# Moving the SBUF pools of a one-core gMLP + SSD block so that the operand tiles begin at multiples of 512 bytes

## The chip, the cores and the metric

The kernel is written for one Trainium2 chip and runs on one of its cores. The core has a matrix engine (TensorE, PE in the profile; its weight loads are listed as PEld), three engines for elementwise work (VectorE = DVE, ScalarE = ACT, GpSimd = POOL) and a queue engine (SyncE = SP) that issues most of the loads; ScalarE issues most of the stores. The metric is the device time of one execution in microseconds. The kernel before takes 1429.13 us, the median of three runs (1428.83 to 1432.63).

## What is computed

One layer over a sequence of 1024 tokens with 1024 features, in float32. The sequence is normalised and modulated, multiplied by a wide input matrix, and its column blocks feed two branches: a gated spatial mixer (y_a) and a chunked state-space scan (SSD, y_b). Both are projected, gated, added, projected once more and normalised.

```
h = rms_norm(x, norm_w) * (1 + scale) + shift        # shift, scale, gate from silu(c) @ ada_w + ada_b
gm_u, gm_v, gm_z, ssm_z, xbc, dt_raw, g_a, g_b = split(h @ w_in)      # 11296 columns
y_a = spatial_gating(gelu(gm_u), gelu(gm_v), ...) * silu(gm_z)
xs, bm, cm = split(silu(causal_depthwise_conv(xbc)))
dt = softplus(dt_raw + dt_bias);  a = -exp(a_log)
y_b = rms_norm((ssd_scan(xs, dt, a, bm, cm) + xs * d_skip) * silu(ssm_z))
merged = sigmoid(g_a) * (y_a @ w_proj_a) + sigmoid(g_b) * (y_b @ w_proj_b)
out = rms_norm(x + gate * (merged @ w_out), final_norm_w)
```

The vectors dt_bias, a_log and d_skip, 32 numbers each (one for each SSD head), are the ones whose tiles the change moves.

## The kernel before

**Products.** The large products are made from two-part operands: a float32 value is split into a rounded high part (type fp32r, which the matrix engine takes in one pass) and a low part, and three products of parts are added (high by high, high by low, low by high). A matmul multiplies a stationary operand of 128x128 (512 bytes on each partition), loaded into the array ahead of it, by a moving operand of 128x512 (2048 bytes on each partition). In the trace the names on the right of the arrow give both, as in xz<-t3h,p7z2h: t3h moves, p7z2h stands still.

**Stages**, in order of time on the core:

1. 0 to 75 us, the first stage. `first_products` (lines 351 to 361) multiplies the first 288 columns while h is made. Its tiles live in the pool p0. The queue's order there is written out: at the second step (n == 1), after the loads of the next modulation block and weights, lines 449 to 451 load dtb, abc and dsk, each a broadcast of 32 numbers to 128 partitions. dsk is read once, in `small_parameters` (line 431), to make dskt.
2. 75 to 930 us, the rest of the input matrix in pairs of column blocks. `product` (line 573) issues 12 matmuls with one of the operands of h (b11, t1, t2, b22, t3, b21, t4; pool hp) moving and one of the weight blocks (pool wp) standing. A pair has seven products. Small tasks are put between products by `later` and `run_tasks`: a task given a delay of n runs n products on. One chain of such tasks, `dt_part1` to `dt_part3`, starts after 216 products: it loads dt_raw back from memory (dtt, line 648), adds dtb (line 663) and, some products later, exponentiates abc (line 690) and multiplies by it (line 692).
3. 930 to 1168 us, the SSD scan, with the projection of y_a (`proj_a`, tile pma) drawn in between in small portions. The order of all engines is written out here (the flag `hand`).
4. 1168 to 1345 us, the projection of y_b: `multiply` (line 1525), 56 units of 12 matmuls. The moving parts (named ..bh and ..bl) are in hp; the stationary blocks (named ..a) come from `big`, which takes 4096-byte places in the pools p2r and p2q.
5. 1345 to 1431 us, the output product (`out_product`, tile po). Its moving operand (woh, wol) is in hp. Its stationary parts come from `m_slot`: fifteen of the 32 lie in five tiles of tag sl (pools p2r and p2q; they appear as mmh and mml), seventeen in single places of hp (mh and ml).

**Pools.** SBUF is laid out as two stacks. The left one grows upward: const, then hp (56 tiles of 2048 bytes), then p0, whose place is taken by wp and wsp (16 and 8 tiles of 2048 bytes) once the first stage is over. The right one grows downward from the top: w4 (six tiles of 4096 bytes), then gm and gx; gx gives way to the pool pre, and later w4, gm and pre give way to p2r, p2x and p2q, which reach down over the places of wsp and wp. A tile that takes a place must wait until those who used the place before are done (`reuse_waits`). The operations that aren't pinned to program order are put in order by the framework's scheduler.

**Where tiles begin.** In the program before, ident, the first tile of const, begins 128 bytes past a multiple of 512. Const holds six tiles of 512 bytes (ident, ones, tri, par, par2, cwt), four of 1024 (dthq, dde, nacs, cd) and small ones: nhalf 32, dtb 128, abc 128, dskt 64, dsk 128, sc 32, ssq 256. That is 7936 bytes, and 128 + 7936 is 384 past a multiple of 512. So hp, and after it wp and wsp, whose tiles all have 2048 bytes, begin 384 past a multiple of 512. The top of the right stack is at 480 past a multiple of 512, and so are all its tiles of 4096, 2048 and 1024 bytes.

Of the kernel before, what the change touches and what calls it, by code (L numbers as in the profile page):

```python
# [8 lines left out]
F32 = mybir.dt.float32  # L9
# [7 lines left out]
P = 128  # L17
# [6 lines left out]
NH = 32  # L24
# [11 lines left out]
def hybrid_kernel(  # L36
# [47 lines left out]
    def cst(shape, name, dt=F32):  # L84
        return const.tile(shape, dt, name=name, tag=name)
# [9 lines left out]
    def f32(t):  # L95
        return t.bitcast(F32)

    def load(dst, src):
        pin(nc.sync.dma_start(dst, src))
# [23 lines left out]
    par = cst([P, P], "par")  # L123
    par2 = cst([P, P], "par2")
    cwt = cst([P, P], "cwt")
    dtb = cst([P, NH], "dtb")
    abc = cst([P, NH], "abc")
    dskt = cst([P, 16], "dskt")
    dsk = cst([P, NH], "dsk")
    sc = cst([P, KT], "sc")  # L130
    dthq = cst([P, NCH * NH], "dthq")
    dde = cst([P, NCH * NH], "dde")
# [30 lines left out]
    def last_split(nm):  # L163
# [2 lines left out]
        pin(A.copy(hi, t))  # L166
        pin(V.tensor_sub(lo, t, f32(hi)))

    w4pool = tc.tile_pool(name="w4pool", bufs=1, side="right", reuse_waits="tile")
    w4p = w4pool.__enter__()  # L170
    w4 = [w4p, 6]

    def wide(name, dt=F32):
        return w4[0].tile([P, S], dt, name=name, tag="w4", bufs=w4[1])


    with tc.tile_pool(name="p0", bufs=1, reuse_waits="tile") as p0:
# [8 lines left out]
        def aw_tile(n):  # L186
            return p0.tile([P, KT, 2, P], F32, name=f"aw{n}", tag="aw", bufs=2)

        hf2 = {}

        def hf_tile(k, h):
# [18 lines left out]
        def load_aw(n):  # L210
            k = KS[n]
            if n:
                aw[n] = aw_tile(n)
            for j in range(2):
                load(aw[n][:, :, j, :],
                     ada_w[:, j * D + k * P : j * D + (k + 1) * P].rearrange("(k p) c -> p k c", p=P))

        def load_w0(n):
            k = KS[n]
            raw = p0.tile([P, W0], F32, name=f"w0r{n}", tag="w0r", bufs=2)  # L220
            wd = p0.tile([P, 2 * NH], F32R, name=f"w0d{n}", tag="w0d", bufs=2)
            hi, lo = (p0.tile([P, 256], F32R, name=f"w0{v}{n}", tag=f"w0{v}", bufs=2) for v in "hl")
            load(raw, w_in[k * P : (k + 1) * P, COL_DT : COL_DT + W0])
            wk[n] = (raw, wd, hi, lo)

        def split_w0(n):
            raw, wd, hi, lo = wk[n]
            pin(A.copy(hi, raw[:, NH:W0]))
            pin(A.copy(wd[:, 0:NH], raw[:, 0:NH]))
            pin(V.tensor_sub(lo, raw[:, NH:W0], f32(hi)))  # L230
            pin(V.tensor_sub(wd[:, NH:], raw[:, 0:NH], f32(wd[:, 0:NH])))
# [119 lines left out]
        def first_products(n):  # L351
            raw, wd, wh, wl = wk[n]
            for h in halves(n):
                hh, hl = hhs[n, h]
                for m, (lw, r) in enumerate(((wh, hh), (wl, hh), (wh, hl))):
                    for i in (1, 2):
                        mm(accs[i][h], lw[:, i * P - P : i * P], r, n + m == 0, n == KT - 1 and m == 2)
                        yield
                for nd, r in ((2 * NH, hh), (NH, hl))[:: 1 if n == 0 else -1]:
                    mm(accs[0][h][0:nd, :], wd[:, 0:nd], r, n == 0 and r is hh, n == KT - 1 and r is hh)  # L360
                    yield
# [46 lines left out]
        def prepare(n):  # L408

            if n == 1:  # L410
                return {
                    8: lambda: (warm(6), transposes(0, 1), rows_of_h(0, 1), matvec(1), warm(5)),
                    11: lambda: (transposes(1, 1), modulation(1), rows_of_h(1, 1)),
                    16: lambda: (transposes(1, 0), rows_of_h(1, 0)),
                }
            a, b = halves(n)
            return {
                2: lambda: (matvec(n), transposes(n, a)),
                6: lambda: (modulation(n), rows_of_h(n, a)),
                14: lambda: (transposes(n, b), rows_of_h(n, b)),  # L420
            }

        def small_parameters():
            pp = ax("pp1")
            for i in range(2):
                tp(pp[:, i * P : (i + 1) * P], pkb[:, i], ident)
            for i in range(2):
                pin(V.tensor_copy((par2, cwt)[i], pp[:, i * P : (i + 1) * P]))
            for hh in range(2):
                part = slice(hh * HD, (hh + 1) * HD)  # L430
                pin(V.tensor_copy(dskt[part, :], dsk.rearrange("p (i h) -> p i h", h=2)[part, :, hh]))
# [10 lines left out]
        for n in range(KT):  # L442
            todo = prepare(n + 1) if n + 1 < KT else {}
            for at, _ in enumerate(first_products(n), 1):
                if at == 1 and n + 2 < KT:
                    load_aw(n + 2)
                    load_w0(n + 2)
                if at == 1 and n == 1:
                    load(dtb, dt_bias.to_broadcast([P, NH]))
                    load(abc, a_log.to_broadcast([P, NH]))  # L450
                    load(dsk, d_skip.to_broadcast([P, NH]))
                if at in todo:
                    todo[at]()
                for f, kk in sums.get((n, at), ()):
                    f(kk)
                if at == 2 and 0 < n < KT - 1:
                    split_w0(n + 1)
                if n == 4 and at == 8:
                    small_parameters()
# [7 lines left out]
    gm = gmpool.__enter__()  # L467
# [23 lines left out]
    def later(delay, f, *a):  # L491
        tasks.append((slot[0] + delay, f, a))
# [143 lines left out]


    bsb = gm.tile([P, D], F32, name="bsb", tag="bsb")
    first_c1 = {"v0": gx.tile([P, S], F32, name="c1v0", tag="wst")}
    wst = None  # L640
    bst = gx.tile([P, NCH, NG, 6], F32, name="bst", tag="bst")
# [3 lines left out]
    def dt_part1():  # L645

        dtt = wide("dtt2")[0 : 2 * NH, :]
        load(dtt, dt_d)
        V.tensor_add(fold[0], ident[:, 0:NH], ident[:, NH : 2 * NH])
        sm1 = wide("sm1").rearrange("p (a n) -> p a n", a=4)  # L650
        sm2 = wide("sm2").rearrange("p (a n) -> p a n", a=4)
        later(2, dt_part1a, dtt, sm1, sm2)
# [522 lines left out]
    def stats():  # L1175
        v_stats()
        mix_load(0)

    later(216, dt_part1)
    later(9, mix_weights)  # L1180
    for i in range(4):
# [586 lines left out]
```

## Time and profile before

| | us |
|---|---|
| median of three runs | 1429.13 |
| the profiled execution, whole | 1432.24 |
| its span, first to last instruction | 1430.5 |
| PE busy within the span | 1400.6 (98%), 7087 matmul records |
| DVE busy | 1027.8 (72%) |
| ACT busy | 782.0 (55%) |
| POOL busy | 204.9 (14%) |

The span is what the trace shows; the profiled execution's own time is 1.7 us longer than it, and 3.1 us longer than the median of the runs. In the trace a matmul's duration runs from its start to a modelled end, and successive matmuls overlap, so a duration is not a pace. The pace is read from starts: a row of the timeline gives the start of a group, its length and how many instructions it merges, and from the start of one group to the start of a later one, divided by the number of matmuls between, is the time that one takes. A granted clock (PEclk) of 1.00 means that the matrix engine was not throttled in that stretch.

### The profile page before, as it was taken

The numbers are of one execution on the slowest core, as the hardware profiler recorded it, in microseconds if no ns is written. First come the engines' busy times: TensorE is split into PE (matmuls) and PEld (weight loads), VectorE is DVE, ScalarE is ACT, GpSimd is POOL, SyncE is SP. The second block draws the span as 40 slices with busy tenths as digits, with TensorE's granted clock in tenths as the row PEclk, the third lists the DMA queues.
The fourth block names the chain that finished last, engine by engine and source line by source line (L and its number), as shares of the span: only waits on it lengthen the run. The fifth ranks groups of instructions, "written<-read, shape, count | busy, mean of one in ns | idle before, by whom it ended". The sixth has DMA issues, their size and how long they took to land.

```text
span 1430.5 us, 20475 instructions
## 1 busy us (share of the span) xinstructions
PE 1400.6 (98%) x7087; PEld 1154.9 (81%) x7087; DVE 1027.8 (72%) x1821; ACT 782.0 (55%) x1444; POOL 204.9 (14%) x190
## 2 busy tenths in 40 slices
PE   8999999999999999999999999989999989999997
PEld 6678888888888888888888888878888878787886
DVE  5686676777667888788887884568878767948443
ACT  6664576566656665555665554757776633325101
POOL 0000000000000000000000100038878830000000
PEclk9999999999999999999999999989999999999999
DMA  8552343333333677597687764788878568977331
GB/s 274 154 163 89 118 118 104 103 103 112 109 110 90 206 224 221 169 266 220 179 248 207 218 188 146 262 289 284 294 263 303 198 229 298 333 259 281 123 118 74
DMA packets 260524, 277.08 MB, mean 194 GB/s; under 512 B 13596, under 2 KB 210628, under 8 KB 260420
## 3 DMA queue, kind: packets, MB, share of 16 engines
q1 hardware_dynamic: 179396, 195.37, 43.4%
q10 hardware_dynamic: 81024, 80.40, 16.6%
q8 instruction: 56, 0.92, 0.3%
q14 instruction: 48, 0.39, 0.1%
HBM read 191.40 MB, written 84.31 MB: 193 GB/s over the span
## 4 chain that ended last, share of the span: by engine, by line
PE 73%; DMA 8%; DVE 6%; ACT 5%; issue 4%; POOL 3%; SPq 1%; ACTq 0%; POOLq 0%; DVEq 0%
PE xuz L573 6%; PE po L90 6%; PE xcb L573 6%; PE xx L573 5%; PE xz L573 5%; PE x L1525 4%; PE yp L1525 3%; PE yuz L573 3%; PE pma L90 3%; PE xv L573 3%; PE ycb L573 3%; PE yx L573 3%; PE xg L573 2%; PE yz L573 2%; DMA yn<-yb_d 2%
## 5 line engine op out<-in xcount | busy, mean ns | idle before, releaser
L780 POOL TENSOR_TENSOR wog<-wog,gb 128x1024 f32<-128x1024 f32 x8 | 22.2, 2773 | 724.9 <-DMA wbr<-in_w_proj_b_dram 569.8
L56 ACT ACTIVATE dcy<-dcy,nacs 128x128 f32<-128x128 f32 x224 | 68.6, 388 | 31.8 <-POOL dcy L56 15.6
L90 PE MATMUL pma<-yh,wah 128*128 128x512 f32 x128 | 44.4, 427 | 1.8 <-ACT bn L1019 1.8
L892 ACT ACTIVATE ac<-ac 128x1024 f32<-128x1024 f32 x32 | 33.9, 1061 | 21.2 <-DVE ac L890 21.1
L1731 ACT ACTIVATE xr<-r 128x1024 f32<-128x1024 f32 x7 | 7.4, 1061 | 67.5 <-issue 39.7
L90 PE MATMUL pma<-yh,wal 128*128 128x512 f32 x128 | 43.6, 422 | 0.0
L56 DVE TENSOR_TENSOR ym<-yn,ea 128x512 f32<-128x512 f32 (+1 forms) x32 | 19.9, 623 | 29.9 <-PE yn L90 29.8
L56 POOL TENSOR_TENSOR yz<-y,sl 128x512 f32<-128x512 f32 x32 | 41.1, 1284 | 0.6
L90 PE MATMUL pma<-yl,wah 128*128 128x512 f32 x128 | 40.9, 401 | 0.0
L1721 POOL TENSOR_TENSOR r<-r,fnw 128x256 f32<-128x256 f32 (+1 forms) x3 | 2.7, 916 | 254.6 <-ACT xr L1720 254.6
L56 POOL TENSOR_TENSOR y<-y,ym 128x512 f32<-128x512 f32 (+1 forms) x32 | 36.5, 1141 | 17.9 <-DVE ym L56 17.9
L56 DVE TENSOR_TENSOR dcy<-dcy,pc 128x1024 f32<-128x1024 f32 x30 | 36.6, 1219 | 2.4 <-PE pc L93 1.4
L890 DVE SCALAR_TENSOR_TENSOR ac<-c2x,cwt,ac 128x1023 f32<-128x1023 f32 (+2 forms) x24 | 31.8, 1325 | 9.0 <-ACT ac L888 7.1
L90 PE MATMUL yi<-dcy,xd 128*64 128x128 f32 x512 | 35.9, 283 | 2.3 <-DVE xe L1013 1.4
L1730 DVE TENSOR_TENSOR r<-po,xr 128x1024 f32<-128x1024 f32 x7 | 8.6, 1225 | 41.1 <-PE po L90 41.1
L1464 DVE SCALAR_TENSOR_TENSOR yn<-yn,par,rb 128x512 f32<-128x512 f32 x32 | 24.5, 765 | 16.0 <-DMA yn<-yb_d 15.9
L56 ACT ACTIVATE ea<-dcy 64x512 f32<-64x512 f32 x56 | 35.2, 629 | 1.3 <-DMA dcy<-acs_d 1.0
L890 DVE SCALAR_TENSOR_TENSOR ac<-c2cb,cwt,ac 128x1023 f32<-128x1023 f32 (+2 forms) x24 | 30.6, 1274 | 7.3 <-ACT ac L888 7.1
L56 POOL TENSOR_SCALAR_AFFINE_SELECT dcy<-dcy 128x1024 f32<-128x1024 f32 x28 | 32.0, 1141 | 18.3 <-ACT ea L56 17.6
L90 PE MATMUL sp<-xe,bn 128*128 128x256 f32 x112 | 33.7, 418 | 0.0
L90 PEld LDWEIGHTS yi<-dcy,xd 128*64 128x64 f32 x512 | 28.1, 139 | 6.9 <-issue 4.7
L56 DVE SCALAR_TENSOR_TENSOR y<-sl,dskt,yi 128x256 f32<-128x256 f32 x64 | 27.7, 473 | 7.7 <-PE yi L90 4.3
(2844 smaller groups left out, 4435.9 us busy)
## 6 DMA issues: line engine op xcount, KB each, us to landing
sl<-s_d SPq DMA_DIRECT2D x32, 768.0 KB
s_d<-ac ACTq DMA_DIRECT2D x32, 512.0 KB
dcy<-acs_d SPq DMA_DIRECT2D x32, 512.0 KB
aw<-in_ada_w_dram SPq DMA_DIRECT2D x16, 512.0 KB
wbr<-in_w_proj_b_dram SPq DMA_DIRECT2D x64, 128.0 KB
wb_d<-wbb ACTq DMA_DIRECT2D x32, 256.0 KB
wb_d<-wbc ACTq DMA_DIRECT2D x32, 256.0 KB
yb_d<-yz ACTq DMA_DIRECT2D x32, 256.0 KB
```

The costliest lines, as they stand in the source:

```text
L56: return lambda *a, **k: tc.keep_in_program_order(f(*a, **k))
L90: pin(PE.matmul(acc, l, r, start=first, stop=last))
L573: pin(PE.matmul(ps, lw[:, k * P : (k + 1) * P], r[k], start=first and n + k == 0, stop=n == 2 and k == 3, skip_group_check=not first))
L780: G.tensor_mul(w, w, gb)
L890: V.scalar_tensor_tensor(ac[:, s:], cc[:, : S - s], conv_wt[:, 3 - s, i : i + 1], ac[:, s:], op0=ALU.mult, op1=ALU.add)
L892: A.activation(ac, ac, AF.Silu)
L1464: V.scalar_tensor_tensor(t, t, snw[:, n : n + 1], rbs[n // 2, h], op0=ALU.mult, op1=ALU.mult)
L1525: pin(PE.matmul(ps[j], a[:, v, js], r, start=first and n + k == 0, stop=n == 2 and k == KT - 1, skip_group_check=not first))
L1721: G.tensor_mul(r[:, cs], r[:, cs], fnw[:, cs])
L1730: V.tensor_add(r, pw, xr)
L1731: A.activation(xr, r, AF.Square, accum_out=sq[:, 0:1])
```

## The change

Five small tiles move and one is added; no arithmetic changes.

- dtb, abc and dsk (128 bytes each) leave const. Const gets 384 bytes shorter, so hp, wp and wsp begin at a multiple of 512 instead of 384 past one.
- A new pool edge takes 480 bytes (one tile of 120 numbers that nobody reads or writes) at the top of the right stack. w4, and with it everything below, moves down by 480 bytes, to multiples of 512.
- dsk becomes a tile of p0, between the x tiles and aw. In p0 the x tiles then begin at a multiple of 512, aw, pk, scz and pkb at 128 past one, w0h and w0l at 384 past one (before: 384, 384 and 128).
- dtb and abc become the first two quarters of a 512-byte tile dta of gm, which keeps the tiles below it at multiples of 512. Their loads go from the first stage (lines 449 and 450) to `dt_part1`, behind the load of dtt. In gx, wst lies 352 past a multiple of 512 (before: 320).
- ident, ones and tri stay where they are, 128 past a multiple of 512.
- The right pools of the later stages move down by 480 and the left ones by 384 bytes. p2x and p2q, which began 96 bytes past a tile border of wsp and wp, now begin on it.

```
@@ -123,10 +123,7 @@
     cwt = cst([P, P], "cwt")
-    dtb = cst([P, NH], "dtb")
-    abc = cst([P, NH], "abc")
     dskt = cst([P, 16], "dskt")
-    dsk = cst([P, NH], "dsk")
     sc = cst([P, KT], "sc")
@@ -166,6 +163,8 @@
+    edge = ctx.enter_context(tc.tile_pool(name="edge", bufs=1, side="right"))
+    edge.tile([P, 120], F32, name="edge", tag="edge")
     w4pool = tc.tile_pool(name="w4pool", bufs=1, side="right", reuse_waits="tile")
     w4p = w4pool.__enter__()
     w4 = [w4p, 6]
@@ -186,6 +185,7 @@
+        dsk = p0.tile([P, NH], F32, name="dsk", tag="dsk")
         hf2 = {}
@@ -446,8 +446,6 @@
                 if at == 1 and n == 1:
-                    load(dtb, dt_bias.to_broadcast([P, NH]))
-                    load(abc, a_log.to_broadcast([P, NH]))
                     load(dsk, d_skip.to_broadcast([P, NH]))
@@ -636,6 +634,8 @@
     bsb = gm.tile([P, D], F32, name="bsb", tag="bsb")
+    dta = gm.tile([P, P], F32, name="dta", tag="dta")
+    dtb, abc = dta[:, 0:NH], dta[:, NH : 2 * NH]
     first_c1 = {"v0": gx.tile([P, S], F32, name="c1v0", tag="wst")}
@@ -646,6 +646,8 @@
         dtt = wide("dtt2")[0 : 2 * NH, :]
         load(dtt, dt_d)
+        load(dtb, dt_bias.to_broadcast([P, NH]))
+        load(abc, a_log.to_broadcast([P, NH]))
         V.tensor_add(fold[0], ident[:, 0:NH], ident[:, NH : 2 * NH])
```

More of the change, by code (lines that the diff above doesn't have):

```diff
@@ L125, in hybrid_kernel @@
     cwt = cst([P, P], "cwt")
-    dtb = cst([P, NH], "dtb")
-    abc = cst([P, NH], "abc")
     dskt = cst([P, 16], "dskt")
-    dsk = cst([P, NH], "dsk")
     sc = cst([P, KT], "sc")
@@ L167, in last_split @@
         pin(V.tensor_sub(lo, t, f32(hi)))
+    edge = ctx.enter_context(tc.tile_pool(name="edge", bufs=1, side="right"))
+    edge.tile([P, 120], F32, name="edge", tag="edge")
     w4pool = tc.tile_pool(name="w4pool", bufs=1, side="right", reuse_waits="tile")
@@ L187, in aw_tile @@
             return p0.tile([P, KT, 2, P], F32, name=f"aw{n}", tag="aw", bufs=2)
+        dsk = p0.tile([P, NH], F32, name="dsk", tag="dsk")
         hf2 = {}
@@ L448, in hybrid_kernel @@
                 if at == 1 and n == 1:
-                    load(dtb, dt_bias.to_broadcast([P, NH]))
-                    load(abc, a_log.to_broadcast([P, NH]))
                     load(dsk, d_skip.to_broadcast([P, NH]))
@@ L638, in hybrid_kernel @@
     bsb = gm.tile([P, D], F32, name="bsb", tag="bsb")
+    dta = gm.tile([P, P], F32, name="dta", tag="dta")
+    dtb, abc = dta[:, 0:NH], dta[:, NH : 2 * NH]
     first_c1 = {"v0": gx.tile([P, S], F32, name="c1v0", tag="wst")}
@@ L648, in dt_part1 @@
         load(dtt, dt_d)
+        load(dtb, dt_bias.to_broadcast([P, NH]))
+        load(abc, a_log.to_broadcast([P, NH]))
         V.tensor_add(fold[0], ident[:, 0:NH], ident[:, NH : 2 * NH])
```

## The prediction

> **What bounds the kernel now.** First the page's part on busy time, then a table of the five stages.
>
> ```profile
> PE 1400.6 (98%) x7087; PEld 1154.9 (81%) x7087; DVE 1027.8 (72%) x1821; ACT 782.0 (55%) x1444; POOL 204.9 (14%) x190
> ```
> ```profile
> core 0: us, PE busy (x) PEld busy (x) DVE busy (x) ACT busy (x) POOL busy (x), PEclk, DMA share, GB/s
> 0.00:75.00 75.00, 67.65 (x473) 50.46 (x474) 43.47 (x107) 49.01 (x91) 3.12 (x10) 1.00 0.69 204
> 75.00:930.00 855.00, 853.23 (x3869) 705.67 (x3867) 647.72 (x1104) 509.46 (x837) 25.47 (x11) 1.00 0.55 166
> 930.00:1168.00 238.00, 231.00 (x1674) 198.69 (x1674) 176.99 (x317) 150.94 (x391) 173.58 (x166) 0.98 0.78 268
> 1168.00:1345.00 177.00, 171.11 (x717) 136.32 (x717) 127.90 (x206) 62.12 (x107) 0.00 (x0) 0.98 0.78 276
> 1345.00:1431.00 86.00, 77.64 (x359) 63.79 (x357) 31.72 (x91) 10.52 (x21) 2.75 (x3) 0.98 0.23 80
> ```
>
> PE is busy 98% of the span at nearly full clock, and no other engine passes 76% of any long stage (DVE, 647.72 of 855). So the time is the number of matmuls times their pace, and the question is whether the pace depends on where operands begin. The PE timeline answers it in three places. First stage 2, where the moving operand (hp) and the stationary one (wp) both begin at 384 past a multiple of 512:
>
> ```profile
> 631.14 1.07 PE L573 MATMUL xz<-t3h,p7z2l 128*128 128x512 f32 x4
> ...
> 657.44 1.07 PE L573 MATMUL xx<-t4l,p4x5h 128*128 128x512 f32 x4
> ```
>
> Between these starts lie 29 groups of four: 26.30 us for 116 matmuls, 226.7 ns each. Then stage 4, moving at 384, stationary at 480:
>
> ```profile
> 1229.64 0.63 PE L1525 MATMUL yp<-p5bh,p5a 128*128 128x512 f32 x2
> ...
> 1234.56 0.63 PE L1525 MATMUL yp<-p5bh,p5a 128*128 128x512 f32 x2
> ...
> 1239.48 0.63 PE L1525 MATMUL yp<-p5bh,p5a 128*128 128x512 f32 x2
> ```
>
> Rows of two and of one alternate: 42 matmuls in 9.84 us, 234.3 ns each. Last, the output product, where one line of code uses stationary blocks from both kinds of place:
>
> ```profile
> 1409.61 0.63 PE L90 MATMUL po<-woh,mml 128*128 128x512 f32 x2
> 1410.08 0.39 PE L90 MATMUL po<-wol,mml 128*128 128x512 f32 x1
> ...
> 1411.02 0.39 PE L90 MATMUL po<-woh,mmh 128*128 128x512 f32 x1
> ...
> 1411.94 0.39 PE L90 MATMUL po<-woh,mh 128*128 128x512 f32 x1
> ...
> 1413.98 0.39 PE L90 MATMUL po<-woh,mmh 128*128 128x512 f32 x1
> ```
>
> From the first to the third of these rows six matmuls with mml and mmh (480) start in 1.41 us, 235 ns each; from the fourth to the fifth nine with mh and ml (384) in 2.04 us, 226.7 ns. The place of the stationary block costs about 7.6 ns a matmul, 3%, and nothing else differs.
>
> **The price of each place.** 480 is a multiple of 32 but not of 64; 384 is a multiple of 128. So the trace shows what 32 past a multiple of 64 costs. It shows no PE operand at a multiple of 512, so what 384 costs against 0 has to be bounded. Both operands of stage 2 move by the same 128 bytes, so their starts stay equal to each other, as before. Its pace also holds while DVE and ACT, busy 76% and 60% of that stage, read and write all over SBUF; what it depends on lies between PE's own two streams. The nearest row is stage 2 itself, equal starts at a multiple of 128, and I take its 226.7 ns for every pair after the change. The two ends:
>
> ```profile
> 122.56 1.88 PE L90 MATMUL prs<-wst,ones 128*128 128x512 f32 x4
> L90 PE MATMUL prs<-wst,ones x4: 593/593/595, 122.6 to 123.9; 128*128 128x512 f32 x4
> ```
>
> These are full float32 passes at half speed: (1.88 - 0.593) / 3 = 429 ns for 512 columns, so 214.5 ns if they ran at full speed with nothing lost. That is the lower end, 12 ns under stage 2. The upper end is 234.3 ns for all, the pace where starts don't suit each other. One page can be set beside the rows: the Trainium skill, TensorE: Matmul & The Clock Gate, section "Wait — 56ns, not 53.3ns?", gives 215.7 ns for back-to-back matmuls of 512 columns; no fp32r row here comes down to it, and by it the sum below would be some 62 us instead of 6.6.
>
> **What the change removes, adds and moves.**
>
> Counts, from a table of whole-span windows for each line or tile:
>
> ```profile
> 0.00:1431.00 1431.00, 829.09 (x3612) 675.62 (x3612) 0.99 0.60 194
> 0.00:1431.00 1431.00, 161.97 (x672) 128.24 (x672) 0.99 0.60 194
> 0.00:1431.00 1431.00, 103.71 (x384) 73.35 (x384) 10.31 (x16) 0.99 0.60 194
> 0.00:1431.00 1431.00, 33.56 (x128) 23.20 (x128) 4.02 (x6) 3.70 (x6) 0.99 0.60 194
> 0.00:1431.00 1431.00, 17.74 (x68) 12.39 (x68) 2.74 (x4) 1.24 (x2) 0.99 0.60 194
> 0.00:1431.00 1431.00, 9.27 (x32) 5.27 (x32) 2.77 (x4) 3.10 (x4) 0.99 0.60 194
> ```
>
> They are line 573 (3612), line 1525 (672), pma (384), mmh (128), mml (68), and the first stage's matmuls that move the parts of b12 out of w4 (32).
>
> 1. Line 1525: 672 x (234.3 - 226.7) = 5.1 us off the path. PE is the bound there, 171.11 of 177 us; DVE at 127.90 and the transfers at 0.78 have room for 3%.
> 2. Output product: 196 x 7.6 = 1.5 us. Twenty-two of these are half as wide; I let them stand at the same price.
> 3. First stage: at most 32 x 7.6 = 0.2 us, but PE waits for engines there (below), so 0.
> 4. Lines 573 and pma, and the output product's other 212: nothing at the price taken. Bounds: 4208 x -12 = -51 us and 4208 x +7.6 = +32 us.
> 5. The two loads: in the first stage they go from between these,
>
> ```profile
> 29.01 0.42 SPq L99 DMA_DIRECT2D dtb<-in_dt_bias_dram  x1
> 29.48 0.42 SPq L99 DMA_DIRECT2D abc<-in_a_log_dram  x1
> 29.95 0.43 SPq L99 DMA_DIRECT2D dsk<-in_d_skip_dram  x1
> 32.24 1.00 SPq L99 DMA_DIRECT2D aw<-in_ada_w_dram  x2
> ...
> 673.03 0.50 SPq L99 DMA_DIRECT2D dtt<-dt_d  x1
> 674.79 0.37 SPq L99 DMA_DIRECT2D a11g<-in_w_in_dram  x1
> L663 DVE TENSOR_TENSOR sm<-pdtt,dtb x1: 418/418/418, 697.3 to 697.3; 128x256 f32<-128x256 f32 x1
> ```
>
> The queue stood idle 1.9 us behind dsk, so taking 0.9 us out ahead of it brings nothing forward. Behind dtt it stands idle 1.26 us (673.53 to 674.79), which covers the two issues of 0.42 us; dtb is read 24 us later, abc later still. Without that cover a11g and the weight loads queued behind it would come 0.9 us late, still hidden by the products before theirs. No gain, no loss.
> 6. edge and dta: no instruction. dsk lies in bytes that the first weight tile of wsp takes over together with aw; aw's last reader, in the loop's seventh step, comes after dsk's, in its fifth, so no new wait.
> 7. New overlaps of p2x and p2q: each tile now lies on one or two old places instead of reaching 96 bytes into a further one, so waits can fall away, not arise. What they could free at the entry to stage 3 is small, since PE's waits are on engines, not on loads:
>
> ```profile
> PE pp L93 <- DMA pk<-in_ada_b_dram: 3.5, 1, 3.5
> PE x L1525 <- DVE tha L1335: 3.5, 1, 3.5
> PE px L93 <- ACT hf L305: 3.0, 4, 0.9
> ```
>
> I take 0, with bounds of -2 us and, as the scheduler may place unpinned work differently around new overlaps, +3.5 us, the longest wait of the list.
> 8. DVE and ACT: the same operation into both kinds of place costs the same.
>
> ```profile
> L1562 ACT CAST mmh<-tg x6: 616/619/622, 1226.4 to 1296.6; 128x512 fp32r<-128x512 f32 x6
> L1562 ACT CAST mh<-tg x8: 616/618/623, 1314.7 to 1337.8; 128x512 fp32r<-128x512 f32 x8
> ```
>
> The sum: -5.1 - 1.5 = -6.6 us, 1432.24 to 1425.6 for the profiled execution. That execution is 3.1 us above the median of the runs, so the median goes from 1429.13 to 1422.5.
>
> **The rivals.**
>
> *The 512 matters too* (operands on such a border run at up to full pace). For it: 12 ns between stage 2 and the half-speed passes are unexplained, and every fp32r operand now lies off a 512 border. Against: starts stay equal to each other. All the way: -51 us of point 4, -672 x 19.8 = -13.3 us and -196 x 19.8 = -3.9 us, to 1361; half way about 1392.
>
> *It does nothing.* Place is then only a companion of something else, such as the order of destinations or of moving operands, the weight loads take nothing from the matmul that runs beside them, and 1429.1 stands. The rows of the output product speak against it, since there only the pool of the stationary tile changes; so does its matmul duration, 389 against 394 ns:
>
> ```profile
> L90 PE MATMUL po<-woh,mh x68: 278/389/506, 1333.6 to 1420.7; 128*128 128x512 f32 x60, 128*128 128x256 f32 x8
> L90 PE MATMUL po<-woh,mmh x77: 277/394/400, 1344.5 to 1422.4; 128*128 128x512 f32 x67, 128*128 128x256 f32 x10
> ```
>
> The Trainium skill, same page, section "Step-by-step: what each phase is for", says that loading the next tile's weights takes no SBUF read bandwidth from the running matmul, which speaks for this rival. The trace disagrees, by those 5 ns.
>
> *Slower: both streams on the same border.* If equal starts at 0 meet each other worse than at 384, stage 2 goes to the pace of stage 4. Its price is +32 us of point 4 with the 6.6 us not gained: 1461; a quarter of it, 1437. It decides from 6.6 us / 4208 = 1.6 ns a matmul upward. For it: 3612 matmuls of the kernel lie at the good place already, so most of it can only be disturbed. Against: the two starts shift together and by a whole 128 bytes.
>
> **How the numbers follow.** The forecast has a chance of 0.56, the 512 rival 0.12, nothing 0.15, slower 0.17. A measurement of this kernel tells about 0.3%, 4.3 us, from no change; the forecast's own 1422.5 lies 6.6 us away, and with point 7's bounds its range is 1420 to 1426, of which 0.04 falls within 0.3%. Faster: 0.52 + 0.12 = 0.64; the same: 0.15 + 0.04 = 0.19; slower: 0.17. The range of 8 in 10 holds the forecast and no change, and reaches into both other cases by about a half: 1395 to 1440.
>
> **What will show it.** Right: line 1525 starts every 227 ns and its matmuls last 389 ns, po shows one pace for mh and mmh, line 573 stays at 226.7, and stage 4 takes 172 us instead of 177. The 512 rival: line 573 under 226 ns. The slower one: line 573 over 228 ns, or irregular. Nothing: L1525 still at 234. I am wrong outright if the paces come out as forecast and the sum is lost again in waits at the entry to stage 3 or 4.

## The result, and the profile after

The changed kernel takes **1423.34 us** (median of 6 runs, 1422.18 to 1426.2) against 1428.71 (6 runs, 1427.86 to 1432.63) for the kernel before beside it: ratio 0.9961, 95% interval 0.9947 to 0.9975. That is 5.4 us less, where 6.6 were forecast. The profiled execution took 1426.2 us, against 1432.24; its span is 1424.5 us, against 1430.5. The page's busy times, after:

```profile
PE 1391.4 (98%) x7087; PEld 1152.5 (81%) x7087; DVE 1026.6 (72%) x1821; ACT 783.4 (55%) x1444; POOL 205.2 (14%) x190
```

All counts of instructions are those of before, and PE is busy 9.2 us less in a span that is 6.0 us shorter, so it also idles 3.2 us more. The table of stretches, after, with the bounds that the prediction used for before (columns as there):

```profile
75.00:930.00 855.00, 853.43 (x3868) 705.70 (x3867) 646.46 (x1104) 509.82 (x834) 25.88 (x11) 1.00 0.54 165
```

In this stretch PE is as busy as before, 853.43 us against 853.23. What moved lies behind it. The same view cut where stage 4 and the output product really begin, in the kernel before

```profile
1165.90:1333.60 167.70, 161.81 (x675) 128.41 (x674) 123.29 (x198) 60.79 (x105) 1.16 (x1) 0.98 0.79 278
1333.60:1430.50 96.90, 89.04 (x409) 73.20 (x407) 38.44 (x103) 13.94 (x27) 2.75 (x3) 0.98 0.28 98
```

and in the changed one:

```profile
1166.80:1328.90 162.10, 155.80 (x676) 126.81 (x676) 122.66 (x198) 60.52 (x105) 1.05 (x1) 0.99 0.81 288
1328.90:1424.50 95.60, 87.76 (x409) 73.19 (x407) 38.41 (x103) 13.95 (x27) 2.75 (x3) 0.97 0.28 99
```

Stage 4 is 5.6 us shorter, the output product 1.3. Against that, stage 4 begins 0.9 us later than before (1166.8 against 1165.9), and 5.6 + 1.3 - 0.9 is the 6.0 us by which the span is shorter. The PE timeline of the changed kernel shows how, at the three places that the prediction read. Stage 2:

```profile
632.39 1.07 PE L571 MATMUL xz<-t3h,p7z2l 128*128 128x512 f32 x4
...
658.69 1.07 PE L571 MATMUL xx<-t4l,p4x5h 128*128 128x512 f32 x4
```

29 groups of four in 26.30 us: 226.7 ns, as before. Stage 4, both operands now on a multiple of 512:

```profile
1224.68 0.62 PE L1527 MATMUL yp<-p5bh,p5a 128*128 128x512 f32 x2
...
1234.20 0.62 PE L1527 MATMUL yp<-p5bh,p5a 128*128 128x512 f32 x2
```

42 matmuls in 9.52 us: 226.7 ns, where there were 234.3. The output product:

```profile
1405.31 0.39 PE L90 MATMUL po<-woh,mh 128*128 128x512 f32 x1
...
1408.03 0.39 PE L90 MATMUL po<-woh,mmh 128*128 128x512 f32 x1
...
1410.52 0.39 PE L90 MATMUL po<-woh,mmh 128*128 128x512 f32 x1
```

Twelve with mh and ml in 2.72 us (226.7 ns), then eleven with mmh and mml in 2.49 us (226.4 ns): one pace for both kinds of place. The tile rows agree: mmh's matmul lasts 389 ns now, as mh's does, where it was 394.

```profile
L90 PE MATMUL po<-woh,mh x68: 278/389/497, 1328.9 to 1414.7; 128*128 128x512 f32 x60, 128*128 128x256 f32 x8
L90 PE MATMUL po<-woh,mmh x77: 279/389/389, 1339.8 to 1416.4; 128*128 128x512 f32 x67, 128*128 128x256 f32 x10
```

### The profile page after: what moved, and what is told of

Its sections match the earlier page's. It is cut to its first block, busy times and chain, and to the rows that moved or that the text cites. A ratio compares the mean times of both kernels' runs of the same rounds, so it can differ in the third digit from the quotient of the medians.

```text
span 1424.5 us, 20475 instructions
## 1 busy us (share of the span) xinstructions
PE 1391.4 (98%) x7087; PEld 1152.5 (81%) x7087; DVE 1026.6 (72%) x1821; ACT 783.4 (55%) x1444; POOL 205.2 (14%) x190
## 4 chain that ended last, share of the span: by engine, by line
PE 80%; DMA 6%; DVE 4%; ACT 3%; issue 3%; POOL 3%; SPq 1%; POOLq 0%; ACTq 0%; DVEq 0%
PE xx L571 6%; PE xuz L571 6%; PE xcb L571 6%; PE po L90 6%; PE xz L571 6%; PE x L1527 6%; PE xg L571 3%; PE pma L90 3%; PE yuz L571 3%; PE yx L571 3%; PE yp L1527 3%; PE xv L571 3%; PE ycb L571 3%; PE yz L571 3%; PE yv L571 2%
```

## The experiments

The theory before these runs was A, that the pace hangs on the difference between the starts of the two operands, at first modulo 64 bytes. Its rivals: B, that a multiple of 512 matters as such; C, that the moved loads or the new overlaps of pools made the gain; D, that each operand by itself must lie on a multiple of 64. In the tables a pace is the mean from start to start over all matmuls of 512 columns whose successor starts within 250 ns, from the raw starts of the trace; a start is given modulo 512.

### One pool of 96 bytes, and one of 32

The kernel before with a single addition, at the top of the right stack:

```
+    edge = ctx.enter_context(tc.tile_pool(name="edge", bufs=1, side="right"))
+    edge.tile([P, 24], F32, name="edge", tag="edge")
```

All operands of stages 2 and 4 then start at 384.

> The kernel before with a 96-byte pool at the top of the right stack: the right stack's tiles begin 384 past a multiple of 512, as hp, wp and wsp already do; const and the loads stay as before. Theory A (the price arises where the two operands of a matmul begin 32 bytes apart modulo 64): line 1525 starts every 227 ns, time 1423.3 us or within 1.5 us of it. Theory B (operands have to begin on a multiple of 512): line 1525 stays at 234 ns, time 1428.7. Theory C (the gain came from the two loads that moved or from the new overlaps): 234 ns, 1428.7.

The second has `[P, 8]`: 384 and 448.

> The kernel before with a 32-byte pool at the top of the right stack: its tiles begin 448 past a multiple of 512, a multiple of 64 but not of 128; hp stays at 384. Theory A: 227 ns in line 1525, 1423.3 us. If 128 is the modulus that matters: line 1525 over 230 ns and 1426 to 1429 us. Theory B: 234 ns, 1428.7.

And the changed kernel without its edge: moving 0, stationary 480 as before.

> The changed kernel without the pool edge: hp, wp and wsp at multiples of 512, the right stack at 480 past one; the loads are moved as in the change. Theory A: line 1525 at 234 ns, time 1428.7 us, no gain. Theory B: half of the operands are on the border, line 1525 between 227 and 234, time 1424 to 1428. Theory C: 1423.3.

| kernel | moving / stationary, stage 4 | median us (runs) | ratio to before [95%] | pace stage 2 | pace stage 4 | pace mmh, mml |
|---|---|---|---|---|---|---|
| before, profiled | 384 / 480 | | | 226.95 | 234.26 | 233.84 |
| after, profiled | 0 / 0 | | | 227.03 | 226.99 | 226.67 |
| 96 bytes | 384 / 384 | 1425.28 (10) | 0.9972 [0.996, 0.9983] | 226.96 | 227.15 | 226.67 |
| 32 bytes | 384 / 448 | 1428.6 (12) | 1.0 [0.9989, 1.001] | 226.95 | 233.30 | 233.28 |
| no edge | 0 / 480 | 1428.52 (12) | 0.9998 [0.9985, 1.001] | 227.01 | 233.31 | 233.01 |

(Paces in ns. Before, on that chip: 1429.34, 33 runs.) The stage 4 timelines, first of the 96-byte kernel, then of the 32-byte one:

```profile
1224.97 0.61 PE L1527 MATMUL yp<-p5bh,p5a 128*128 128x512 f32 x2
...
1237.21 0.61 PE L1527 MATMUL yp<-p5bh,p5a 128*128 128x512 f32 x2
```
```profile
1225.20 0.63 PE L1527 MATMUL yp<-p5bh,p5a 128*128 128x512 f32 x2
...
1239.20 0.63 PE L1527 MATMUL yp<-p5bh,p5a 128*128 128x512 f32 x2
```

54 matmuls in 12.24 us (226.7 ns) against 60 in 14.00 us (233.3 ns). Equal starts at 384 give stage 4 the full pace with no operand on a multiple of 512, so B falls for this gain, and neither the loads nor dsk were touched. The time is 4.1 us under its own before, though 1425.28 lies half a microsecond above what was expected. The overlaps of pools are not separated here: with both stacks at 384, p2x and p2q begin on a tile border just as in the change. The 32-byte pool was a miss: a difference of 64 bytes should have counted as equal, and gained nothing. So the modulus is not 64.

### The difference, or each operand by itself

The kernel before with 32 bytes more at the end of const:

```
     ssq = cst([P, NG * NCH], "ssq")
+    cst([P, 8], "fill")
```

Stage 2 has both operands at 416, 32 past a multiple of 64; stage 4 has 416 and 480.

> The kernel before with 32 more bytes in const: hp, wp and wsp begin 416 past a multiple of 512, the right stack 480 past one. Every operand of lines 573 and 1525 is then 32 past a multiple of 64, and equally so. Theory A (only the difference counts): both lines at 227 ns, 1423.3 us. Theory D (each operand by itself has to begin on a multiple of 64): line 573 at 234 ns or more, 3612 x 7.6 = 27 us, 1456 us. Theory B: as before, 1428.7.

Measured: 1429.18 us (12 runs), ratio 1.0003 [0.9993, 1.0012]. The timeline of this kernel, stage 2 and then stage 4:

```profile
632.03 1.07 PE L574 MATMUL xx<-b11h,p1x5h 128*128 128x512 f32 x4
...
657.42 1.07 PE L574 MATMUL xx<-t4l,p4x5h 128*128 128x512 f32 x4
```
```profile
1223.95 0.63 PE L1526 MATMUL yp<-p5bh,p5a 128*128 128x512 f32 x2
...
1238.65 0.63 PE L1526 MATMUL yp<-p5bh,p5a 128*128 128x512 f32 x2
```

Stage 2 keeps its pace (28 groups, 112 matmuls, in 25.39 us: 226.7 ns) with both operands off every multiple of 64: D falls, and it is the difference of the two starts that counts, not either start. Stage 4 misses its expectation in the same way as the 32-byte pool: 63 matmuls in 14.70 us, 233.3 ns at a difference of 64. From here on A said modulo 256, to be tested by streams alone (below).

### Stage 2 made unequal; the loads alone

The kernel before with 32 bytes between hp and wp, so that stage 2 has 384 and 416:

```
+    gap = tc.tile_pool(name="gap", bufs=1)
+    gap.__enter__().tile([P, 8], F32, name="gap", tag="gap")
...
+    gap.__exit__(None, None, None)
```

> The kernel before with a 32-byte pool between hp and wp: in line 573 the moving operand begins at 384 and the stationary one at 416 past a multiple of 512; line 1525 stays as it was (384 and 480). Theory A: line 573 goes from 227 to 234 ns, 3612 x 7.6 = 27 us, time 1456 us. Theory B (only the border of 512 counts, off it all places cost the same): 1428.7.

And the kernel before with only the loads of dtb and abc moved, a filler in their old place, so that every start is as before:

```
-    dtb = cst([P, NH], "dtb")
-    abc = cst([P, NH], "abc")
+    cst([P, 2 * NH], "fill")
...
-                    load(dtb, dt_bias.to_broadcast([P, NH]))
-                    load(abc, a_log.to_broadcast([P, NH]))
...
+    dta = gm.tile([P, P], F32, name="dta", tag="dta")
+    dtb, abc = dta[:, 0:NH], dta[:, NH : 2 * NH]
...
+        load(dtb, dt_bias.to_broadcast([P, NH]))
+        load(abc, a_log.to_broadcast([P, NH]))
```

> The kernel before with the loads of dtb and abc moved as in the change (tile dta in gm, loads behind that of dtt) and a filler of 256 bytes in their place in const, so that hp stays at 384 and the right stack at 480. Theory A: no gain, 1428.7 us within 1.5. Theory C: 1423.3.

The gap costs: 1448.89 us (4 runs) against 1428.83 (17 runs), ratio 1.0134 [1.0111, 1.0156], 20 us. Its stage 2 on the timeline:

```profile
637.13 1.10 PE L575 MATMUL xz<-t2l,p6z2h 128*128 128x512 f32 x4
...
663.26 1.10 PE L575 MATMUL zx<-b21h,p2x5l 128*128 128x512 f32 x4
```

28 groups in 26.13 us: 233.3 ns. The pace alone makes 3612 x (233.32 - 226.95) = 23 us; what gaps of over 250 ns between starts cost in that stage fell by 1.8 us, which leaves 21. The expectation was higher because it took the 234.3 ns of a difference of 96 for one of 32. The loads alone do nothing: 1429.37 us (12 runs), ratio 0.9996 [0.9984, 1.0009], paces 226.90, 234.23 and 233.84 as before. C falls as far as the loads go. The overlaps of pools come together with the equal starts in every kernel here, so no kernel tests them alone; against them speaks that the gain is one of pace, which streams without any of these pools show as well (below).

### Streams at chosen places

Two kernels that hold nothing but streams of matmuls, fp32r except where said. The loop of the second (the first has no `cols` and no `pair`):

```
        for i in range(n):
            k = i % 4
            pin(nc.tensor.matmul(t[0:cols, 0:w], pair[1][:, k * P + o : k * P + o + cols],
                                 pair[0][:, k * 512 + m : k * 512 + m + w], start=i == 0, stop=i == n - 1))
```

In fp32r the stationary tile begins 4 x o bytes, the moving one 4 x m bytes past a multiple of 512.

> Not the layer: one load, four copies and 20 streams of 48 fp32r matmuls back to back on one moving and one stationary tile, both at a multiple of 512; the streams differ in the bytes by which they begin past it (w...: stationary; m...: moving; both...: both). The output is zeros, nothing of the layer is computed. Theory A: 227 ns for wzero, wsixtyfour, wonetwentyeight, wtwofiftysix, msixtyfour, bothsixtyfour and boththirtytwo; 234 ns for wthirtytwo, wninetysix and mthirtytwo; in between or other for offsets that are no multiple of 32. Theory B: 227 or less for wzero alone, slower for all others. If the 12 ns above 215 come from the weight load beside the matmul, the half-wide stream starts every 107 + 2 + 10 to 13 = 119 to 122 ns.

The timeline of the first one; names beginning with w shift the stationary operand by that many bytes, those with m the moving one. The pace is the row's length, less the 0.39 us of its last matmul, over 47 steps.

```profile
20.30 11.05 PE L63 MATMUL wzero<-mov,sta 128*128 128x512 f32 x48
...
75.71 11.35 PE L63 MATMUL wthirtytwo<-mov,sta 128*128 128x512 f32 x48
...
109.30 11.36 PE L63 MATMUL wsixtyfour<-mov,sta 128*128 128x512 f32 x48
120.50 11.40 PE L63 MATMUL wninetysix<-mov,sta 128*128 128x512 f32 x48
131.74 11.32 PE L63 MATMUL wonetwentyeight<-mov,sta 128*128 128x512 f32 x48
142.90 11.05 PE L63 MATMUL wtwofiftysix<-mov,sta 128*128 128x512 f32 x48
153.78 11.28 PE L63 MATMUL msixteen<-mov,sta 128*128 128x512 f32 x48
...
176.10 11.15 PE L63 MATMUL msixtyfour<-mov,sta 128*128 128x512 f32 x48
...
198.24 11.08 PE L63 MATMUL boththirtytwo<-mov,sta 128*128 128x512 f32 x48
...
220.06 11.05 PE L63 MATMUL samew<-mov,sta 128*128 128x512 f32 x48
230.96 5.91 PE L63 MATMUL half<-mov,sta 128*128 128x256 f32 x48
```

That is 226.8 ns at a difference of 0, 233.2 at 32, 233.4 at 64, 234.3 at 96, 232.6 at 128, and 226.8 again at 256. The layer's own paces come back without the layer: 234.3 at 96 (before), 233.3 at 64 and 32. Shifting the moving operand by 64 gives 228.9, not the 233.4 of the stationary one: the sign of the difference counts, as 256 - 64 = 192 would have it. Both shifted by 32 is a difference of 0 again (227.5 with its slower first matmuls). The 227 ns that were expected at differences of 64 and 128 are misses.

Two streams say something of the 12 ns above 215. The half-wide one moves 256 columns and starts a matmul every 119.8 ns (5.91 us, less 0.28, over 47 steps), inside the 119 to 122 named for it. Half of the 215.9 that bf16 takes below would be 108, so some 12 ns are lost there too: by these two widths the loss comes once per matmul and not per column. And samew, which loads one and the same block for all 48, still runs at 226.8, so the loss does not come from one block following another.

The second walks the difference from 0 to 252 in steps of 4, to see whether some place is faster than 0. Its streams of differences are of 40 matmuls, so 39 steps; the streams at the end, of 48, lie at a difference of 0 modulo 256, but for bfnear at 48 (not shown: as bffar) and bffar at 96.

> Not the layer: the streams on one moving and one stationary tile again, nothing of the layer computed, output zeros. 64 streams of 40 matmuls: the stationary operand begins 0, 4, 8 ... 252 bytes past the moving one (names daa to dhh, two letters a to h counting in eights and ones); then stationary operands of 128, 64 and 32 columns at difference 0, and three bf16 streams at differences 0, 48 and 96 bytes. Theory A, mended after the first runs (only the difference of the starts modulo 256 bytes counts, and 0 is its best value): daa 226.7 ns, all others 228 to 235. Rival E: some difference runs under 226.7 ns, down to 215, and stage 2 can still be sped up by a pool shifted by that much. If the 12 ns over 215 are what the weight load takes from the moving stream: 220 ns with 64 columns, 217 with 32, and about 216 for bf16 at all three differences, since its streams ask for half the bytes; if they belong to the change of weights itself: 227 for all.

```profile
20.92 9.24 PE L69 MATMUL daa<-mov,sta 128*128 128x512 f32 x40
...
253.44 9.23 PE L69 MATMUL ddb<-mov,sta 128*128 128x512 f32 x40
...
401.22 9.66 PE L69 MATMUL dfb<-mov,sta 128*128 128x512 f32 x40
...
466.60 9.32 PE L69 MATMUL dga<-mov,sta 128*128 128x512 f32 x40
...
577.99 9.30 PE L69 MATMUL dhe<-mov,sta 128*128 128x512 f32 x40
...
605.77 9.23 PE L69 MATMUL dhh<-mov,sta 128*128 128x512 f32 x40
614.84 11.06 PE L69 MATMUL colsfull<-mov,sta 128*128 128x512 f32 x48
625.74 11.20 PE L69 MATMUL colshalf<-mov,sta 128*64 128x512 f32 x48
636.78 11.28 PE L69 MATMUL colsquarter<-mov,sta 128*32 128x512 f32 x48
647.90 10.53 PE L69 MATMUL bfzero<-mob,stb 128*128 128x512 bf16 x48
...
668.63 10.52 PE L69 MATMUL bffar<-mob,stb 128*128 128x512 bf16 x48
```

Seven of the 64 streams take 9.23 to 9.25 us, some 226.8 ns a matmul: differences of 0 (daa), 100 (ddb), 120, 144, 156, 228 and 252 (dhh). The other 57 take 9.29 to 9.66 (dfb, a difference of 164), 228 to 238 ns; 192 (dga), the place of the first kernel's msixtyfour, is at 229.0 again. That some places other than 0 run at full pace was not expected. None is under the pace of equal starts, so no layout of this kernel's fp32r operands found here beats it, and rival E falls. The difference is not quite all, though: at 240 the first kernel, which gets there by shifting the moving operand by 16 (msixteen), takes 231.7 ns and this one (dhe) 228.5. What is shown is that equal starts reach full pace in every stream and every long stage here; why an unequal pair costs what it costs is not.

### The whole change and the 96 bytes on one chip; dsk elsewhere

Again the changed kernel, and the 96-byte kernel, sharing the runs of before; with them the changed kernel with dsk placed behind the weight tiles of p0:

```
-        dsk = p0.tile([P, NH], F32, name="dsk", tag="dsk")
         hf2 = {}
...
+        dsk = p0.tile([P, NH], F32, name="dsk", tag="dsk")
         sq0 = p0.tile([P, NCH], F32, name="sq0", tag="sq0")
```

> The changed kernel once more, to have it on the chip of the next two. Theory A: 5 to 6 us under the kernel before.

> The kernel before with the 96-byte pool alone, on the chip of the changed kernel. Theory A: the same time as the changed kernel within 1 us, since every pair of operands of lines 573, 1525, pma and po begins equally in both. If a start at 512 is worth anything in addition, for transfers or for waits between pools: the changed kernel is 1 to 3 us ahead.

> The changed kernel with dsk behind w0l in p0 instead of between x and aw, so that w0h and w0l begin 256 past a multiple of 512 and no longer 384 past one, against hp at 0. Theory A with modulus 256: the 96 matmuls of 512 columns in the first stage go from a difference of 128 to one of 0 and take up to 96 x 5 = 0.5 us less; not to be told apart from the changed kernel. If the modulus were 64: the same time and the same starts as the changed kernel.

| kernel | median us (runs) | ratio to before [95%] | pace first stage | pace stage 2 | pace stage 4 | pace mmh, mml |
|---|---|---|---|---|---|---|
| after | 1425.85 (9) | 0.9976 [0.9966, 0.9985] | 233.0 | 227.03 | 226.96 | 226.70 |
| 96 bytes | 1424.6 (7) | 0.997 [0.9958, 0.9982] | 231.6 | 226.94 | 227.02 | 226.67 |
| after, dsk elsewhere | 1426.34 (12) | 0.9975 [0.9961, 0.9989] | 231.0 | 227.02 | 226.95 | 226.65 |

(Before: 1429.27, 23 runs.) The changed kernel is 3.4 us under before here, where 5 to 6 were expected, and its median is 1.25 us above that of the 96 bytes, where 1 was allowed for; but their intervals overlap from 0.9966 to 0.9982, so the two can't be told apart. Nothing that these runs could see is left for 512-byte borders or the moved loads; the overlaps of pools are the same in both. Putting dsk elsewhere speeds the first stage's undisturbed matmuls up by 2 ns, at most 0.2 us over 96 of them, and the time doesn't show it. They stay at 231.0 although their starts are now equal. What may hold them there is that equal starts don't run at full pace at once: the first stage issues most of these matmuls in runs of two to eight, and in the changed kernel's pma, whose starts are equal too, the second to tenth matmul of a portion average 230.1 ns and those from the eleventh on 226.7.

## Why the prediction was right, and where it wasn't

The path was right (PE's pace in stage 4 and in the output product) and the sum nearly so; the reason for the price was right where it spoke of the two starts together and wrong where it spoke of each alone. Point by point:

1. **Line 1525** (term 5.1 us). The pace went from 234.26 to 226.99: 672 x 7.27 = 4.9 us. Stage 4 itself lost 5.6 us in the profiled pair, but such a length scatters by some 4 us with the waits: over the five profiled executions with equal starts it is 162.1 to 166.2 us. The pace is the firm part. (The 177 and 172 us of the prediction are not the stage: their stretch begins 2 us late and takes in 11 us of the output product.)
2. **Output product** (1.5 us). 172 undisturbed matmuls of mmh and mml gained 7.17 ns each, 1.2 us, and 186 of mh and ml 0.6 ns each, 0.1 us. The stretch lost 1.3. Half as wide are 24 of the 196, not twenty-two.
3. **First stage** (0). Its pace got slightly worse, 232.26 to 233.08, since w0h lies at another distance from its moving operand. Stage 2 begins 1.0 us later (74.7 to 75.7), and 75.6 and 75.3 in the two other executions with dsk in p0, against 74.0 to 75.3 in the eight layer kernels without dsk there or without the edge. Moving dsk within p0 didn't bring it back, so whether that microsecond is more than scatter, and its cause, stay open.
4. **Line 573, pma, the rest of po** (0 with bounds of -51 and +32 us). 226.95 to 227.03, 230.17 to 229.73, and the rest as in 2: equal starts that stay equal cost the same at 384, at 416 and at 0. That pma stays at some 230 is the slow start of its short portions (above). The lower bound halved the 429 ns of full float32 passes; that these run at exactly half speed no run shows, but bf16's 215.9 ns comes near its 214.5. Both rivals that hung on this point, the 512 gain and the clash on the border, needed another pace here, and fall with it.
5. **The two loads** (0, covered by 1.26 us in which the queue was idle). The price was wrong and the cover was elsewhere. The timeline of SP's queue, after:

```profile
673.59 0.50 SPq L99 DMA_DIRECT2D dtt<-dt_d  x1
675.23 0.35 SPq L99 DMA_DIRECT2D dta<-in_dt_bias_dram  x1
679.06 0.35 SPq L99 DMA_DIRECT2D dta<-in_a_log_dram  x1
679.51 0.38 SPq L99 DMA_DIRECT2D a11g<-in_w_in_dram  x1
```

The two issues did not fill the gap behind dtt: they went out where a11g and the load after it had gone (1.64 and 5.47 us behind dtt, where those went 1.76 and 5.69 behind it), and a11g went out 5.92 us behind dtt where it was 1.76, 4.2 us later and not 0.9. Idle time on a queue was not free room there: before and after alike, the profile puts the 1.0 to 1.1 us behind dtt, and the 3.5 us behind the next load, down to waits for earlier stores (th_d<-c1g, wb_d<-wbb) to land. The delay cost nothing all the same, because a11g and dta were not needed yet; a11g is first read at 692.4 us, and dta here:

```profile
L665 DVE TENSOR_TENSOR sm<-pdtt,dta x1: 418/418/418, 698.5 to 698.5; 128x256 f32<-128x256 f32 x1
```

The kernel with the loads alone, level with before, shows it by itself.

6. **edge, dta, dsk** (0). Nothing seen beyond point 3.
7. **New overlaps** (0, from -2 to +3.5). PE's longest waits, after:

```profile
PE pp L93 <- DMA pk<-in_ada_b_dram: 3.6, 1, 3.6
PE x L1527 <- DVE tha L1337: 3.5, 1, 3.5
PE px L93 <- ACT hf L305: 3.0, 4, 0.9
PE yi L90 <- DVE xe L1015: 2.5, 1, 2.5
```

The first three stand as they stood, to 0.1 us; the fourth was 1.4 and now is 2.5.

8. **DVE and ACT** (0). Busy 1026.6 and 783.4 us against 1027.8 and 782.0.

By the paces the sum is 4.9 + 1.3 = 6.2 us, near the forecast 6.6; the medians, in five comparisons (after twice, the 96 bytes twice, dsk elsewhere), show 5.4, 3.4, 4.1, 4.7 and 2.9. So the comparison that answers the prediction is the most favourable of the five. The last two stages together take 257.7 to 261.8 us (mean 259.4) in five profiled executions with equal starts, and 262.4 to 265.4 (mean 264.1) in the three with a difference of 96: 4.7 us. So about 1.5 us of what PE gains seems to go back into waits, which is less than the scatter of one execution; no single wait was found for it.

**The step that failed**, though the number came out, is the reading of the place: "480 is a multiple of 32 but not of 64; 384 is a multiple of 128. So the trace shows what 32 past a multiple of 64 costs." The number of the term was right and the reason wrong. Both operands 32 past a multiple of 64 run at full pace; a difference of 64, a multiple of 64, runs at 233.3. What 234.3 is the price of is 480 - 384 = 96 bytes between the two starts. Had the change put the right stack on a multiple of 64 only, that sentence would have forecast a gain, and the 32-byte pool got none. What saved the forecast was the other sentence, that equal starts stay equal, and some luck: the change puts both operands on a multiple of 512 and so makes them equal too, and either reading forecasts the same gain from it.

The rival that nothing happens leaned on the rule in the Trainium skill, TensorE: Matmul & The Clock Gate, "Step-by-step: what each phase is for", that a weight load takes no read bandwidth from the running matmul. The bf16 streams bear it out as far as place goes (10.53 and 10.52 us at differences of 0 and 96 bytes), and from start to start bffar's matmuls take 215.9 ns, beside the 215.7 of that page's section "Wait — 56ns, not 53.3ns?". The fp32r streams do not: their pace moves with the start of the stationary operand, and never came below 226.6 ns. Whether it is the reading of the weights that holds the moving stream up was not isolated.

## What to carry to other kernels

Where fp32r matmuls follow each other back to back in runs of well over ten, let the stationary and the moving operand begin at the same address modulo 256 bytes, or at least read the pace from start to start (226.7 or 233 to 234 ns here) before laying pools out; it was 3% of the pace of the matmuls concerned, and one pool of 96 bytes gave all of what this change gave. Judge a place by the difference of the two starts and not by what power of two divides each. Before taking a queue's idle time for room, look at what it waits for: here the idle time was itself a wait, and a load put into it moved all that came after. Then see whether what is behind it has time.

## What was not expected of the hardware

The dependence is irregular: equal starts are best, but so are differences of 100, 144 or 252 bytes, beside neighbours at 233 ns, and about half of the places (30 of 64) cost the same 6.6 ns. The cost does not go by how much the weight load reads: stationary tiles of 64 and 32 columns, whose loads last 134 and 109 ns, ran at 230.0 and 231.7 ns, slower than 227.0 for 128 columns at the same place, whose loads last 188. So the 11 ns between fp32r's best pace and bf16's 215.9 are not explained by these runs, and no place gave them back.
